# A decoder block on one core: list schedule with other costs, and four of eight groups of the first MLP layer as seven block products

## The chip, the cores and the metric

One core of one Trainium2 chip. The metric is the device time of one execution in microseconds (us), the median of several runs. Everything is float32; there are no collectives.

## The reference, cut to what matters

A decoder block for 512 tokens and 1024 channels, one layer: a conditioning vector gives shifts, scales and gates; a mixer (convolution branch and attention branch, merged by gates) and then an MLP each add to the residual stream.

```python
h = rms_norm(x, g_pre_mix) * (1.0 + scale1) + shift1
y = token_mixer(h, ...)                          # convolution (31 taps), latent attention (8 heads), output projection
x = x + gate1 * rms_norm(y, g_post_mix)
h = rms_norm(x, g_pre_mlp) * (1.0 + scale2) + shift2
y = jnp.square(jax.nn.relu(h @ w_mlp_in)) @ w_mlp_out     # (512 x 1024)(1024 x 4096), then (512 x 4096)(4096 x 1024)
x = x + gate2 * rms_norm(y, g_post_mlp)
```

In the token mixer the latent rows are normed as `rms_norm(q_lat)` (384 wide) and `rms_norm(kv_lat)` (256 wide); that is `lat_norm` in the kernel.

## The kernel before, in words

**Matmuls.** Every large product is made in three passes: both operands are split into a high part in the rounded type float32r (a cast, on ACT) and a low part (value minus high part, a subtraction on DVE); `mm3` (L454) adds high*high, high*low and low*high. Class `W` (L472) splits a loaded weight tile of 1024 words a partition: one cast on ACT, one subtraction on DVE. Split operands live in `r_arena` (28000 words a partition), unsplit data and loaded weights in `f_arena` (22400 words); PSUM has 8 banks.

**Order.** The program is first only recorded: each operation becomes an `Op` with a cost by `Planner.cost` (L217), its regions read and written by `region` (L195), and its dependencies (`record`, L245). `plan` (L306) is a list scheduler: it gives each operation a deadline, counted back from the PE operations that need it, and lets five queues (PE, ACT, DVE, POOL, SP) run in simulated time; PE takes what is ready in program order, the others by deadline (less a bonus `hurry`). DMA is modelled by 475 ns of issue and one channel of 360 bytes per ns. `lives` (L366) gives the times from which to which each buffer was in use; the arenas place buffers by them in the next pass. After at most `PASSES` passes (L47, L1603) the shortest plan is issued, one instruction after another, by `issue` (L385): hence all instructions have line L388. Each engine runs its queue in that order. A pass that finds no room in an arena ends the search.

```python
    for _ in range(PASSES):
        try:
            plan = emit(plan.lives(), {})
        except MemoryError:
            break
        plan.plan()
        if plan.length < best.length:
            best = plan
```

**The MLP.** `h2` (L1406 and after) holds the normed and modulated tokens as 8 split pairs of 128 channels x 512 tokens: 8192 words of `r_arena`. Tokens come in two halves (`tp`), each of 4 x 2 PSUM pieces of 256 columns; a piece is scaled on ACT, cast on ACT and subtracted on DVE. The hidden layer is worked in four chunks of 8 blocks of 128 hidden channels (`for ch`, L1527). In a chunk:
- the first layer takes two groups of four blocks (8 groups in all; chunk 0 takes four blocks at a time, the others two and two). A block is 8 channel tiles x 3 matmuls of 512 token columns; a group is loaded by four DMAs of 512 KB (`hid_weights`, L1369) and split as four `W`. ACT then takes relu out of PSUM and squares. The very first group runs in two steps of 256 columns, since the second half of the tokens is ready later.
- the second layer of the chunk (512 tokens x 1024 hidden x 1024 channels) is made by `strassen` (L1447): both operands in 2 x 2 blocks, seven products of blocks in place of eight, with sums of blocks formed on DVE in `f_arena` and split afterwards. A product is 2 x 4 x 3 = 24 matmuls of 512 columns and has three split pairs of 1024 words as its operands (one of the hidden values, two of the weights), which are given back after it; `banked` adds its result out of PSUM to the output rows, on DVE or, the first time, by a copy on ACT.

**lat_norm** (L867): for each of four token tiles two squares with a sum (ACT), two scalings (ACT), two powers of -1/2 (POOL, one column each), two multiplies (ACT); then transposes on PE.

The functions that the diff touches:

Of the kernel before, what the change touches and what calls it, by code (L numbers as in the profile page):

```python
# [17 lines left out]
P = 128  # L18
# [28 lines left out]
PASSES = 8  # L47
LEAD = 15000.0
ADAS = (1, 1, 0, 4)
# [117 lines left out]
class Planner:  # L167
# [6 lines left out]
    def __init__(self, nc, spaces):  # L174
        self.spaces = spaces
        self.real = dict(pe=nc.tensor, act=nc.scalar, dve=nc.vector, pool=nc.gpsimd, sp=nc.sync)
        self.ops = []
        self.last_w = {}
        self.reads = {}
        self.boost = 0  # L180
        self.hurry = 0.0
        self.after = None

# [11 lines left out]
    def region(ap):  # L195
# [5 lines left out]
        if row == 0 or len(t.shape) < 2 or "dram" in name or "spill" in name:  # L201
            return name, range(0, 1)
# [5 lines left out]
        return name, range(lo // u, hi // u + 1)  # L208

# [7 lines left out]
    def cost(self, eng, fn, outs, ins, k):  # L217

        n = max(self.free_size(o) for o in (ins if fn == "reduce_sum" else outs))
        if fn == "dma_start":  # L220
            return 475.0, 2000.0
        psum = any(r.tensor.name.startswith("psum") for r in ins + outs)
        if eng == "pe":
            if fn == "transpose":
                return 0.85 * n + 1, 190.0
            if ins[0].dtype == F32:
                return max(53.5, n / 2.4 + 2) * 4, 190.0
            return max(64.0, n / 2.4 + 2.5), 190.0
        scalars = sum(isinstance(v, bass.AP) and self.free_size(v) == 1 for v in ins) if n > 1 else 0
        if eng == "act":  # L230
            t = 0.833 * n + (51 if psum else 93) + 93 * scalars
# [13 lines left out]
    def record(self, eng, fn, a, k):  # L245
# [16 lines left out]
        o.cost, o.post = self.cost(eng, fn, outs, ins, k)  # L262
        if fn == "dma_start":
            b = 4
            for _, c in outs[0].ap:
                b *= c
            o.dma = b
# [38 lines left out]
    def plan(self):  # L306
# [8 lines left out]
        for o in reversed(ops):  # L315
            lat = o.post + (o.dma / 180.0 if o.dma else 0.0)
# [5 lines left out]
        dma_free = 0.0  # L322
        future = []
# [10 lines left out]
        while len(order) < len(ops):  # L334
# [3 lines left out]
            for e in self.NAMES:  # L338
                if free[e] <= now and heaps[e]:
# [53 lines left out]
def tile_hybrid_block(  # L393
# [48 lines left out]
    def emit(past, replay):  # L442
# [424 lines left out]
        def lat_norm():  # L867
            for t in range(NT):
                s = stat(4)
                j = ra.alloc(QL)  # L870
                act.activation(ra.v(j), fa.v(latF[t])[:, 0:QL], AF.Square, accum_out=s[:, 0:1])
                act.activation(ra.v(j)[:, 0:KL], fa.v(latF[t])[:, QL:QL + KL], AF.Square, accum_out=s[:, 1:2])
# [3 lines left out]
                act.mul(fa.v(latF[t])[:, 0:QL], fa.v(latF[t])[:, 0:QL], s[:, 2:3])  # L876
                act.mul(fa.v(latF[t])[:, QL:QL + KL], fa.v(latF[t])[:, QL:QL + KL], s[:, 3:4])
# [472 lines left out]
        h2 = []  # L1350
# [23 lines left out]
        for tp in range(2):  # L1374
# [30 lines left out]
            if tp == 0:  # L1405
                h2[:] = [pair(T) for _ in range(KD)]  # L1406
            hsl = slice(tp * 256, (tp + 1) * 256)
            for k2 in range(KD // 2):
# [5 lines left out]
                for q in range(2):  # L1414
                    k = 2 * k2 + q
                    ps, v = pb.v(b)[:, q * 256:(q + 1) * 256], fa.alloc(256)
                    hb, lb = h2[k]
                    if k == 0:
                        act.activation(ra.v(hb)[:, hsl], ps, AF.Identity, scale=mod[:, 3, k:k + 1], bias=mod[:, 2, k:k + 1])
                        dve.tensor_scalar(fa.v(v), ps, mod[:, 3, k:k + 1], mod[:, 2, k:k + 1], ALU.mult, ALU.add)  # L1420
                    else:
                        act.activation(fa.v(v), ps, AF.Identity, scale=mod[:, 3, k:k + 1], bias=mod[:, 2, k:k + 1])
                        act.copy(ra.v(hb)[:, hsl], fa.v(v))
                    dve.tensor_tensor(ra.v(lb)[:, hsl], fa.v(v), rf(hb)[:, hsl], ALU.subtract)
                    fa.free(v)
# [100 lines left out]

        for ch in range(NCH):  # L1527
# [3 lines left out]
            for n0 in range(0, HPC, GRP):  # L1531
                bs = [pb.alloc() for _ in range(GRP)]
# [17 lines left out]
            if ch == NCH - 1:  # L1550
                for p_ in h2:
# [92 lines left out]
```

## Time and profile before

| | |
|---|---|
| runs, us | 822.37, 822.44, 826.56 |
| median, us | 822.44 |
| the profiled execution, us | 821.15 |
| its span (first to last instruction), us | 819.4 |
| busy, us (share of the span) | PE 799.6 (98%), DVE 685.5 (84%), ACT 423.3 (52%), POOL 28.5 (3%) |
| PE instructions | 3934 matmuls seen |
| DMA | 117.28 MB, mean 143 GB/s |
| granted TensorE clock | 0.997 of full speed |

PE is TensorE's matmuls, PEld its weight loads (which overlap them), DVE is VectorE, ACT ScalarE, POOL GpSimd, SP the engine whose queue issues the DMAs. All times below are counted from the first instruction of the span. Matmuls are pipelined: the duration of one in a row is longer than the distance from its start to the next one's. The profiler misses a few matmuls, so counts of them can be a little low.

### The profile page before, as it was taken

Reading aid. Unit: us, or ns where it says so; the run is one execution under the profiler, and the core shown is the slowest. Engines: PE = TensorE matmul, PEld = TensorE weight load, DVE = VectorE, ACT = ScalarE, POOL = GpSimd, SP = SyncE. Lnnn points to the kernel's source line nnn. Section 1 sums busy time; section 2 is a strip of 40 time slices with the busy share of each in tenths; the row PEclk is TensorE's granted clock in tenths of the full one; section 3 lists DMA queues with packets and bytes.
Section 4 is the critical chain, followed back from the end, with each engine's and each line's share of the span. In section 5 each row is a group of like instructions: output and inputs, shape, how many; then the busy total and the mean of one; then the engine's idle time right before and its main releaser. Section 6 shows DMA issues by size and latency. Waiting matters only on the chain.

```text
span 819.4 us, 10628 instructions
## 1 busy us (share of the span) xinstructions
PE 799.6 (98%) x3934; PEld 673.5 (82%) x3934; DVE 685.5 (84%) x1014; ACT 423.3 (52%) x714; POOL 28.5 (3%) x84
## 2 busy tenths in 40 slices
PE   6999999999999999999999989999999999999995
PEld 4778988899988888888888889888888888888884
DVE  4989899999999999989999798397539993975696
ACT  5373554375894255228334496465345434553552
POOL 2001210000000000000000020000000000000001
PEclk9999999999999999999999999999999999999998
DMA  9997324202263151134799660173015831660302
GB/s 305 330 336 256 126 76 122 80 1 77 79 206 103 27 154 52 52 98 154 255 325 385 239 188 26 52 227 108 0 52 165 283 117 52 201 209 1 103 0 104
DMA packets 87111, 117.28 MB, mean 143 GB/s; under 512 B 7345, under 2 KB 61970, under 8 KB 87058
## 3 DMA queue, kind: packets, MB, share of 16 engines
q1 hardware_dynamic: 87058, 116.59, 44.1%
q8 instruction: 31, 0.51, 0.3%
q14 instruction: 22, 0.18, 0.1%
HBM read 108.18 MB, written 8.39 MB: 142 GB/s over the span
## 4 chain that ended last, share of the span: by engine, by line
PE 95%; ACT 2%; DVE 1%; POOL 1%; DMA 0%; issue 0%; DVEq 0%; ACTq 0%
PE psum L388 95%; DVE f_arena L388 1%; ACT f_arena L388 1%; POOL stats L388 1%; ACT r_arena L388 0%; DMA f_arena<-in_x_dram 0%; ACT stats L388 0%; DVEq L1639 0%; DVE mod L388 0%; ACTq L388 0%
## 5 line engine op out<-in xcount | busy, mean ns | idle before, releaser
L388 PE MATMUL psum<-r_arena 128*128 128x512 f32 (+2 forms) x3592 | 761.5, 372 | 3.2 <-ACT r_arena L388 3.1
L388 PEld LDWEIGHTS psum<-r_arena 128*128 128x128 f32 x3592 | 632.5, 188 | 114.8 <-ACT r_arena L388 3.8
L388 DVE TENSOR_TENSOR r_arena<-f_arena,r_arena 128x1024 fp32r<-128x1024 f32 (+4 forms) x234 | 247.7, 1081 | 92.1 <-PE psum L388 57.6
L388 ACT CAST r_arena<-f_arena 128x1024 fp32r<-128x1024 f32 (+4 forms) x224 | 210.2, 959 | 179.4 <-PE psum L388 117.8
L388 DVE SCALAR_TENSOR_TENSOR f_arena<-f_arena,cw 128x512 f32<-128x512 f32 x240 | 164.9, 744 | 0.0
L388 ACT ACTIVATE f_arena<-psum 128x512 f32<-128x512 f32 x64 | 38.1, 597 | 120.0 <-PE psum L388 119.8
L388 DVE TENSOR_TENSOR f_arena<-f_arena 128x1024 f32<-128x1024 f32 (+3 forms) x78 | 77.0, 1003 | 5.8 <-ACT f_arena L388 3.6
L388 ACT ACTIVATE f_arena<-f_arena 128x512 f32<-128x512 f32 (+4 forms) x100 | 58.5, 604 | 18.6 <-DVE f_arena L388 17.4
L388 DVE SCALAR_TENSOR_TENSOR f_arena<-f_arena,cT 128x256 f32<-128x256 f32 (+2 forms) x84 | 55.3, 699 | 0.1
L388 PE MATMUL psum<-ident,f_arena 128*128 128x128 f32 x234 | 34.9, 286 | 7.6 <-DVE f_arena L388 7.6
L388 PEld LDWEIGHTS psum<-ident,f_arena 128*128 128x128 f32 x234 | 28.8, 147 | 13.0 <-DVE f_arena L388 8.4
L388 DVE TENSOR_TENSOR f_arena<-psum,f_arena 128x512 f32<-128x512 f32 x52 | 35.5, 684 | 4.6 <-PE psum L388 4.4
L388 DVE TENSOR_TENSOR r_arena<-psum,r_arena 128x512 fp32r<-128x512 f32 (+2 forms) x57 | 35.7, 656 | 1.7 <-ACT r_arena L388 1.0
L388 POOL TENSOR_TENSOR stats<-stats,nhalf 128x1 f32<-128x1 f32 x24 | 20.1, 842 | 476.2 <-ACT stats L388 476.2
L388 ACT CAST r_arena<-psum 128x512 fp32r<-128x512 f32 (+2 forms) x57 | 30.1, 566 | 11.1 <-PE psum L388 10.7
L388 ACT COPY f_arena<-psum 128x512 f32<-128x512 f32 (+5 forms) x42 | 19.8, 500 | 17.6 <-PE psum L388 17.6
L388 ACT ACTIVATE r_arena<-f_arena 128x512 fp32r<-128x512 f32 (+3 forms) x20 | 13.0, 651 | 18.3 <-DVE f_arena L388 16.0
L388 DVE CUSTOM_DVE_ANT_0 f_arena<-psum,mask 128x128 f32<-128x128 f32 (+3 forms) x32 | 15.2, 485 | 2.7 <-PE psum L388 2.5
L388 ACT ACTIVATE f_arena<-f_arena,lnh 128x512 f32<-128x512 f32 x16 | 12.2, 808 | 6.8 <-DVE f_arena L388 6.7
L388 DVE TENSOR_SCALAR f_arena<-f_arena,stats 128x1024 f32<-128x1024 f32 x8 | 6.0, 751 | 10.5 <-POOL stats L388 10.5
L388 DVE SCALAR_TENSOR_TENSOR f_arena<-f_arena 128x512 f32<-128x512 f32 (+1 forms) x18 | 13.2, 743 | 0.2 <-ACT f_arena L388 0.2
L388 DVE SCALAR_TENSOR_TENSOR f_arena<-f_arena,psum 128x512 f32<-128x512 f32 x16 | 10.7, 679 | 0.0
(94 smaller groups left out, 180.3 us busy)
## 6 DMA issues: line engine op xcount, KB each, us to landing
f_arena<-in_w_ada_dram SPq DMA_DIRECT2D x16, 1024.0 KB, 5.3
f_arena<-in_w_mlp_in_dram SPq DMA_DIRECT2D x32, 512.0 KB, 4.4
f_arena<-in_w_mlp_out_dram SPq DMA_DIRECT2D x32, 512.0 KB, 5.4
f_arena<-in_w_in_dram SPq DMA_DIRECT2D x24, 512.0 KB, 4.1
f_arena<-in_x_dram SPq DMA_DIRECT2D x8, 512.0 KB, 5.4
f_arena<-in_w_ada_dram SPq DMA_DIRECT2D x16, 256.0 KB, 5.6
f_arena<-in_w_ada_dram SPq DMA_DIRECT2D x8, 512.0 KB, 7.1
h_spill<-r_arena SPq DMA_DIRECT2D x16, 256.0 KB, 3.8
```

Source lines behind the costliest of these rows:

```text
L388: getattr(self.real[o.eng], o.fn)(*o.a, **o.k)
```

## The change

First, the scheduler's model:
- a matmul of n columns costs max(109, n/2.4 + 13.3) ns in place of max(64, n/2.4 + 2.5); a float32 one of a single column 213 ns; ACT's sine 900 ns more.
- a DMA takes 375 ns of issue, and time on its channel by the contiguous run of its access pattern (`run`); at most eight are in flight (`DEPTH`): the SP queue is held until the eighth last has landed.
- DRAM tensors and spills are told apart by offset (`region`), so pieces that don't overlap no longer depend on each other in the plan.
- up to 14 passes in place of 8; operations on POOL recorded while `plan.slack` is set count as done 4 us later.

Second, `lat_norm` squares all four tiles first and takes one scaling and one power of eight columns.

Third, in four of the eight groups of the first MLP layer (`SIN`: the second group of chunk 0, both of chunk 1, the second of chunk 2) `strassen_in` makes the group by seven products of 2 x 2 blocks: 256 hidden x 512 channels by 512 channels x 256 tokens. Each takes 2 x 4 x 3 matmuls of 256 columns. To that end the modulated tokens are also kept unsplit (`h2f`, two tiles of 2048 words of `f_arena`) until `h2_sums` has made four sums of token blocks, each split into a pair of 1024 words (`h2s_`), which stay until the last such group. The weight sums are made for each group on DVE, and its results are put together by copies (ACT), adds out of PSUM (DVE) and relu and square (ACT). The loads of a group stay four of 512 KB.

```diff
-PASSES = 8
+SIN = ((0, 4), (1, 0), (1, 4), (2, 4))
+DEPTH = 8
+PASSES = 14
 LEAD = 15000.0
+SLOW = 4000.0
...
-            return name, range(0, 1)
+            return name, range(ap.offset, ap.offset + 1)
...
-            return 475.0, 2000.0
+            return 375.0, 2000.0
...
-                return max(53.5, n / 2.4 + 2) * 4, 190.0
-            return max(64.0, n / 2.4 + 2.5), 190.0
+                return (213.0 if n == 1 else max(53.5, n / 2.4 + 2) * 4), 190.0
+            return max(109.0, n / 2.4 + 13.3), 190.0
...
+        o.post += self.slack if eng == "pool" else 0.0
...
-            o.dma = b
+            n = min(self.run(outs[0]), self.run(ins[0]), 4096)
+            o.dma = b * (13.0 + 0.0385 * n) / (16 * n)
...
-            lat = o.post + (o.dma / 180.0 if o.dma else 0.0)
+            lat = o.post + (2.0 * o.dma if o.dma else 0.0)
...
-                        dma_free = st + o.dma / 360.0
-                        o.t1 = dma_free + 910.0
+                        dma_free = st + o.dma
+                        o.t1 = dma_free + 1100.0
+                        landed.append(o.t1)
+                        free[e] = max(free[e], landed[-DEPTH])
...
         def lat_norm():
+            s = stat(4 * NT)
             for t in range(NT):
-                s = stat(4)
...
-                rstd(s[:, 2:3], s[:, 0:1], 1.0 / QL)
-                rstd(s[:, 3:4], s[:, 1:2], 1.0 / KL)
...
+            plan.slack = SLOW
+            rstd(s[:, 2 * NT:], s[:, :2 * NT], 1.0)
+            plan.slack = 0.0
...
+                h2f[:] = [fa.alloc(4 * T) for _ in range(2)]
...
+        def h2_sums():
+            Y = {(j, i): k4(fa.v(h2f[j]))[:, :, 256 * i:256 * i + 256] for j in range(2) for i in range(2)}
+            for nm, o, a, b in ((3, (0, 1), (1, 1), (0, 1)), (1, (0, 0), None, (0, 0)), (2, (1, 1), (1, 1), (0, 0)),
+                                (4, (1, 0), (1, 0), (1, 1))):
+                if nm == 1:
+                    dve.tensor_tensor(Y[0, 0], Y[1, 1], Y[0, 0], ALU.subtract)
+                    dve.tensor_tensor(Y[0, 0], Y[0, 0], Y[0, 1], ALU.subtract)
+                else:
+                    dve.tensor_tensor(Y[o], Y[a], Y[b], ALU.subtract)
+                hl = pair(1024)
+                act.copy(k4(ra.v(hl[0])), Y[o])
+                dve.tensor_tensor(k4(ra.v(hl[1])), Y[o], k4(rf(hl[0])), ALU.subtract)
+                h2s_[nm] = hl
+            fa.free(*h2f)
...
+        def strassen_in(hv, n0, c0):
...
+            def product(xb, y, b, first):
+                w = W(fa.v(xb, "p (k n) -> p k n", k=4), 4, 256)
...
+                for m in range(2):
+                    for k in range(4):
+                        mm3(pb.v(b)[:, m * 256:(m + 1) * 256], w(k, m * P, P), ys_[k], first and m == 0 and k == 0, k == 3,
+                            skip_group_check=True)
+                w.free()
...
+            def keep(i, n, b):
+                act.copy(o(i, n), ps(b))
+
+            def done(i, n, b):
+                v = o(i, n)
+                dve.tensor_tensor(v, ps(b), v, ALU.add)
+                act.activation(v, v, AF.Relu)
+                act.activation(v, v, AF.Square)
+
+            x11, x12 = x_(0, 0), x_(0, 1)
+            ba, bb, bc_ = (pb.alloc() for _ in range(3))
+            product(x11, (0, 0), ba, True)
+            keep(0, 0, ba)
+            product(x12, (1, 0), bc_, True)
+            done(0, 0, bc_)
+            pb.free(bc_)
+            x21, x22 = x_(1, 0), x_(1, 1)
+            s1, s2 = fa.alloc(1024), fa.alloc(1024)
+            sub(s1, x21, x22, ALU.add)
+            sub(s2, s1, x11)
+            product(s2, 2, ba, False)
+            keep(0, 1, ba)
+            product(s1, 1, bb, True)
+            fa.free(s1)
+            keep(1, 1, bb)
+            sub(x21, x11, x21)
+            fa.free(x11)
+            product(x21, 3, ba, False)
+            fa.free(x21)
+            done(1, 1, ba)
+            sub(x12, x12, s2)
+            fa.free(s2)
+            product(x12, (1, 1), bb, False)
+            fa.free(x12)
+            done(0, 1, bb)
+            pb.free(bb)
+            product(x22, 4, ba, False)
...
             for n0 in range(0, HPC, GRP):
+                if (ch, n0 - n0 % 4) in SIN:
+                    if n0 % 4 == 0:
+                        if not h2s_:
+                            h2_sums()
+                        strassen_in(hv, n0, (ch * HPC + n0) * P)
...
+                    continue
```

## Rows read from the trace of the kernel before

**Rows 1.** The page, busy us (share of the span) and instructions of each engine.

```profile
span 819.4 us, 10628 instructions
...
PE 799.6 (98%) x3934; PEld 673.5 (82%) x3934; DVE 685.5 (84%) x1014; ACT 423.3 (52%) x714; POOL 28.5 (3%) x84
```

**Rows 2.** The chain that ended last, in order: start us, us, what.

```profile
by line: PE psum L388 94.9%; DVE f_arena L388 1.4%; ACT f_arena L388 0.9%; POOL stats L388 0.7%; ACT r_arena L388 0.4%; DMA f_arena<-in_x_dram 0.4%; issue 0.3%; ACT stats L388 0.1%; DVEq L1639 0.1%; DVE mod L388 0.0%; ACTq L388 0.0%
...
7.19 36.36 PE psum L388 x174
...
44.81 197.30 PE psum L388 x1131
...
242.77 190.97 PE psum L388 x866
...
434.91 23.97 PE psum L388 x112
...
481.39 329.38 PE psum L388 x1545
```

**Rows 3.** Windows: stretch, its us, busy us (instructions) by engine, PEclk, DMA share, GB/s.

```profile
280.00:300.00 20.00, 20.00 (x90) 16.57 (x89) 19.66 (x26) 8.52 (x10) 0.00 (x0) 1.00 0.54 160
...
320.00:340.00 20.00, 20.00 (x90) 16.57 (x89) 20.00 (x30) 5.45 (x7) 0.00 (x0) 1.00 0.10 27
...
460.00:480.00 20.00, 18.09 (x88) 14.41 (x87) 14.18 (x18) 11.73 (x28) 4.79 (x7) 1.00 0.43 146
```

**Rows 4.** Timeline of PE, end of the MLP: start us, us, operation, count.

```profile
799.49 11.27 PE L388 MATMUL psum<-r_arena 128*128 128x512 f32 x49
```

**Rows 5.** Timeline of PEld, first group of the MLP (256 columns a matmul).

```profile
481.39 7.50 PEld L388 LDWEIGHTS psum<-r_arena 128*128 128x128 f32 x62 [0.25 <-DVE f_arena L388]
```

**Rows 6.** Groups by form, PEld: count | busy us, mean ns | idle before.

```profile
L388 PEld LDWEIGHTS psum<-r_arena 128*128 128x128 f32 x3592 | 632.5, 188 | 114.8 <-ACT r_arena L388 3.8 <-DVE r_arena L388 0.5 <-issue 0.4
```

**Rows 7.** Timeline of DVE: subtractions of 1024 words, multiplies of 512.

```profile
500.52 4.63 DVE L388 TENSOR_TENSOR f_arena<-f_arena 128x1024 f32<-128x1024 f32 x4
...
563.54 3.72 DVE L388 TENSOR_TENSOR r_arena<-f_arena,r_arena 128x1024 fp32r<-128x1024 f32 x3 [0.99 <-ACT f_arena L388]
...
800.68 1.88 DVE L388 TENSOR_TENSOR f_arena<-f_arena 128x512 f32<-128x512 f32 x3
```

**Rows 8.** Timeline of ACT: a pass out of PSUM, casts.

```profile
510.67 0.60 ACT L388 ACTIVATE f_arena<-psum 128x512 f32<-128x512 f32 x1 [3.06 <-PE psum L388]
...
531.07 2.01 ACT L388 CAST r_arena<-f_arena 128x1024 fp32r<-128x1024 f32 x2
```

**Rows 9.** Windows by stages of the MLP, engines in the order of rows 3.

```profile
core 0: us, PE busy (x) PEld busy (x) DVE busy (x) ACT busy (x) POOL busy (x), PEclk, DMA share, GB/s
489.00:565.80 76.80, 76.80 (x405) 66.33 (x404) 56.45 (x58) 47.52 (x68) 0.00 (x0) 1.00 0.36 112
565.80:647.40 81.60, 81.60 (x362) 67.57 (x361) 54.74 (x55) 38.96 (x46) 0.00 (x0) 1.00 0.31 97
647.40:729.00 81.60, 81.60 (x362) 67.57 (x361) 64.90 (x65) 40.58 (x46) 0.00 (x0) 1.00 0.49 159
609.30:647.40 38.10, 38.10 (x170) 31.55 (x169) 36.49 (x39) 23.15 (x23) 0.00 (x0) 1.00 0.59 187
489.00:527.70 38.70, 38.70 (x237) 34.78 (x236) 22.31 (x26) 20.15 (x37) 0.00 (x0) 1.00 0.09 25
481.40:810.60 329.20, 329.20 (x1545) 276.42 (x1545) 241.67 (x247) 172.16 (x228) 2.67 (x3) 1.00 0.34 109
```

**Rows 10.** Waits, who for whom: us in total, times, longest us.

```profile
DVE r_arena L388 <- PE psum L388: 57.6, 14, 14.1
```

**Rows 11.** The page, DMA issues: count, KB each, median us to landing.

```profile
f_arena<-in_w_mlp_in_dram SPq DMA_DIRECT2D x32, 512.0 KB, 4.4
```

**Rows 12.** Groups of POOL: count | busy us, mean ns | idle before.

```profile
L388 POOL TENSOR_TENSOR stats<-stats,nhalf 128x1 f32<-128x1 f32 x24 | 20.1, 842 | 476.2 <-ACT stats L388 476.2
L388 POOL TENSOR_TENSOR lns<-lns,nhalf 128x4 f32<-128x4 f32 x1 | 1.4, 1407 | 253.9 <-DVE lns L388 253.9
```

More of the change, by code (lines that the diff above doesn't have):

```diff
@@ L182, in __init__ @@
         self.after = None
+        self.slack = 0.0
     class Engine:
@@ L208, in region, with run @@
         return name, range(lo // u, hi // u + 1)
+    @staticmethod
+    def run(ap):
+        dims = [list(d) for d in ap.ap]
+        if ap.tensor.name.split("_bitcast")[0].endswith("arena") or dims[0][0] == 0:
+            dims = dims[1:]
+        n = 1
+        for s, c in reversed(dims):
+            if s != n:
+                break
+            n *= c
+        return 4 * n
     @staticmethod
@@ L322, in plan @@
         dma_free = 0.0
+        landed = [0.0] * DEPTH
         future = []
@@ L1349, in emit, with k4 @@
             xr.append(b)
-        h2 = []
+        h2, h2f, h2s_ = [], [], {}
+        def k4(a):
+            return a.rearrange("p (k t) -> p k t", k=4)
         def yl(t, k):
@@ new lines, in strassen_in, with x_, sub, o @@
+        def strassen_in(hv, n0, c0):
+            def x_(i, j):
+                return load(1024, w_mlp_in[512 * j:512 * j + 512, c0 + 256 * i:c0 + 256 * i + 256]
+                            .rearrange("(k p) n -> p k n", p=P), "p (k n) -> p k n", k=4)
+            def sub(o, a, b, op=ALU.subtract):
+                dve.tensor_tensor(fa.v(o), fa.v(a), fa.v(b), op)
+            def product(xb, y, b, first):
+                w = W(fa.v(xb, "p (k n) -> p k n", k=4), 4, 256)
+                if isinstance(y, tuple):
+                    ys_ = [h2s(4 * y[0] + k, 256 * y[1], 256) for k in range(4)]
+                else:
+                    ys_ = [tuple(k4(ra.v(q))[:, k] for q in h2s_[y]) for k in range(4)]
+                for m in range(2):
[3 more added lines that the diff above has]
+                w.free()
+            def o(i, n):
+                return hv[:, n0 + 2 * i:n0 + 2 * i + 2, 256 * n:256 * n + 256]
+            def ps(b):
+                return pb.v(b, 512, "p (m t) -> p m t", m=2)
+            def keep(i, n, b):
[33 more added lines that the diff above has]
+            product(x22, 4, ba, False)
+            fa.free(x22)
+            v = o(1, 0)
+            act.activation(v, ps(ba), AF.Relu)
+            act.activation(v, v, AF.Square)
+            pb.free(ba)
@@ L1531, in emit @@
             for n0 in range(0, HPC, GRP):
+                if (ch, n0 - n0 % 4) in SIN:
[3 more added lines that the diff above has]
+                        strassen_in(hv, n0, (ch * HPC + n0) * P)
+                        if ch >= NCH - 2:
+                            take(late, 2 * ADAS[1])
+                        if (ch, n0) == SIN[-1]:
+                            for nm in list(h2s_):
+                                ra.free(*h2s_.pop(nm))
+                    continue
                 bs = [pb.alloc() for _ in range(GRP)]
@@ L1550, in emit @@
             if ch == NCH - 1:
-                for p_ in h2:
+                for p_ in h2 + list(h2s_.values()):
                     ra.free(*p_)
```

27 lines of the change are left out of this document (14 added, 13 removed).

## The prediction

> **What bounds the kernel now.** I read the page's busy times first: PE is busy 98% of the span, DVE 84%, ACT 52% [rows 1]. A busy PE need not be at its peak, so the chain that ended last came next. It is PE for 95%, in three long stretches, and the pieces between them are short: 1.26 us up to 44.81 us, 0.66 at 242 us, 1.17 at 434 us, and a change of hands between ACT, POOL and DVE from 458.9 to 481.4 us, in which PE itself stood still for 20.00 - 18.09 = 1.9 us [rows 2, 3]. Then I asked how fast PE goes where it doesn't wait: 49 matmuls of 512 columns in 11.27 us, the last of them 0.39 us long, so (11.27 - 0.39) / 48 = 226.7 ns from start to start [rows 4]; at 256 columns 62 weight loads, one per matmul, in 7.50 us, the last 0.19 us, so 7.31 / 61 = 119.8 ns [rows 5]. From 481.39 us on, 329.38 us of chain are PE without a break [rows 2]: the MLP is bound by the number and width of matmuls, and nothing waits there. The first matmul comes at 7.19 us, the last ends at 810.77 of 819.4.
>
> **1. Seven products in place of eight.** A group of four blocks took 4 x 8 x 3 = 96 matmuls of 512 columns: 96 x 226.7 = 21.76 us. Now it takes 7 products x 2 x 4 x 3 = 168 of 256 columns: 168 x 119.8 = 20.13 us. The work falls by an eighth (2.72 us), but the narrower form gives 1.09 us back. Four groups: -4 x 1.63 = **-6.5 us**, all on the path, since PE sets the end there. The first group of the MLP already runs this form (same operands, 256 columns), so the price is measured, not guessed.
>
> A rule against this edit: what if each weight load stuck out behind a stream that short? One load lasts 188 ns [rows 6], and if each were waited for, a group would take 168 x 188 = 31.6 us. The row shows 119.8 from start to start, shorter than one load, so loads overlap. The Trainium skill, "TensorE: Matmul & The Clock Gate", section "LDWEIGHTS (loading the stationary operand)", gives about one column per 1.2 GHz cycle, and its section on weight-path modes leaves fp32 out of the fast load. By that the load alone is about 107 ns (an estimate from that page), as long as the stream, and uncovered it would turn the gain into a loss; the trace's 119.8 ns says it is covered.
>
> **2. What DVE and ACT get to do.** DVE prices by start to start: a 128x1024 subtraction (4.63 - 1.22) / 3 = 1.14 us, a 512-column one (1.88 - 0.68) / 2 = 0.60 us [rows 7]. Each changed group adds three low halves (7 splits for 4), four block sums and three adds out of PSUM: 7 x 1.14 + 3 x 0.6 = 9.8 us. The token sums, made once in chunk 0, add 5 subtractions and 4 low halves: 9 x 1.14 = 10.3 us. In all 49.5 us. ACT: 16 more casts at 2.01 / 2 = 1.0 us and 12 more passes of 512 columns at 0.6 us, 23.2 us [rows 8]; it is busy 172 us of the last 329 [rows 9], so this hides behind PE; a cast that came late would cost what a late low half costs, below.
>
> Whether DVE hides too is the question of this case. I cut the MLP at its stages (a group 21.8 us, a second layer 38.1 us, counted back from the last matmul) and asked for the busy times of each stretch [rows 9]:
> - Chunk 0, 489.0 to 565.8: DVE 56.45 us of 76.8. After: 56.5 + 20.1 = 76.6 in 75.2. **Over its room by 1.4 us.**
> - Chunk 1: 54.7 of 81.6. After: 74.3 in 78.3, 95%.
> - Chunk 2: 64.9 of 81.6, after 74.7 in 80.0, 93%; 8 of its operations feed the last gate alone and can slip into chunk 3.
> What cover there is: from 320 to 340 us DVE is busy 20.00 of 20 us and PE 20.00 too, so a full DVE alone does not stop PE; from 460 to 480 us DVE is busy only 14.18 [rows 3], 5.8 us into which sums and splits could move; and the last three subtractions of chunk 0, 3.7 us from 563.54 us on [rows 7], split weights for chunk 1 and can slip. Bounds: at the best 0. At the worst DVE gets 97% of the time, as in 280 to 300 us (19.66 of 20) [rows 3], so chunk 0 lacks 76.6 - 0.97 x 75.2 = 3.7 us, and chunk 1, with these 3.7 us put on it, 78.0 - 0.97 x 78.3 = 2.0 us: 5.7 us. I take **+1.5 us**, nearer to the lower end, because in chunk 1 of before the second layer ran DVE at 36.49 of 38.1 with PE dense [rows 9].
>
> **3. Room for operands.** The first layer's weights come by the same four 512 KB loads per group, same 1 KB runs. But the four token sums hold 8 x 1024 words of the 28000 of r_arena from chunk 0 to the last changed group, in chunk 2, beside 8192 for h2: 11 tiles of 1024 stay, where there were 19. A second-layer product takes 6. That leaves five of the next product's six to be written early; DVE already waits on PE for such tiles 14 times, 57.6 us in all, the longest 14.1 us [rows 10]. Taken at 0; with the cover gone it is the third rival. The float copy of h2 holds 4096 of f_arena's 22400 words until the token sums are made; loads that this puts off have room, with the DMA engines at a share of 0.09 there [rows 9]: 0, and if not, a 512 KB load of 4.4 us [rows 11] late once. In the first layer a PSUM bank is written again after one product on another bank: 24 x 119.8 = 2.9 us of cover for one 0.6 us eviction.
>
> **4. The list schedule.** Its costs now say 226.6 ns for a matmul of 512 columns where they said 215.8, its DMA knows run lengths and eight in flight, and DRAM regions no longer chain transfers that don't touch. Deadlines and places change in the whole kernel, queues of SP and POOL included. The trace of before can't price this. Upper bound of the gain: the breaks above, 1.26 + 0.66 + 1.17 + 1.9 = 5.0 us. Bound of the loss: breaks as large as the ones there are, 5.0 us, since the same kind of order made them. I take **-1.0 us**: PE is dense over 197 and 191 us already, so nothing more is to be had there, and the break at 458.9 to 481.4 is a chain of dependent small steps that no order shortens.
>
> **5. lat_norm.** 8 ACT scalings and 8 POOL powers of one column become one each of eight; a one-column power takes 0.84 us, one of four columns 1.41 [rows 12], so eight in one go take about 2.2 us, against 6.7. It lies under the conv stage, where POOL idles and PE has its next tiles. All four tiles now wait for one power, some 2 us longer for the first; the GLU products in PE's queue cover that, and without them it would cost these 2 us once: 0. The 4 us that the plan books on top of that power only move its users back in the order.
>
> **6. The tail**, 8.6 us behind the last matmul [rows 2], keeps its operations; a row multiply of 0.6 us [rows 7] may change places with another, either way: 0.
>
> **Sum.** -6.5 + 1.5 - 1.0 = -6.0. The profiled execution lasted 821.15 us (span 819.4), so 815.15 for it; the median of the runs is 822.44, 1.29 above the profiled one. Against the median: **816.4 us**. Faster or slower by 0.5% is 4.1 us, about what a measurement of this kernel can tell.
>
> **Rivals.**
> - *The schedule takes all breaks too.* -6.5 - 5.0 = -11.5: 811 us. For it: the costs are now those of the trace. Against: the breaks are dependencies. Chance 0.14.
> - *DVE becomes the bound of chunks 0 and 1.* With the full 5.7 us lost and nothing from the schedule: 822.44 - 6.5 + 5.7 = 821.6, no change. For it: 76.6 us of work in 75.2. Against: the idle 5.8 us before. Also here: the search ends at the first pass that finds no room, and keeps an early order. Chance 0.21.
> - *Operands no longer fit (slower).* The sixth tile of a product is freed when the running product has read its first weights for the last time, 6 matmuls or 1.36 us before its end, and is read 7 matmuls or 1.59 us into the next: 2.95 us for one low half of 1.14. Two DVE operations ahead of it in the queue make 3.42, 0.5 late; three make 4.56, 1.6 late. Two and three in turn, over the 14 products of chunks 0 and 1: 14 x 1.05 = 14.7 us, 822.44 - 6.5 + 14.7 = 830.6. It decides from 0.76 us per product (10.6 / 14). For it: DVE would be 95% busy, and its queue is in order. Against: before, with six more tiles in reserve, no PE gap at all. The Trainium skill, "Perfetto Trace Analysis", section "Optimization Strategy", reads one gap that repeats on the busiest engine as a sign that the next tile had no room; no such gap is in this trace. Chance 0.11.
> - *Weight loads uncovered* (above): +39 us. Chance 0.01.
>
> **How the numbers follow.** The forecast (816.4, its own range 814 to 819) has 0.53. Faster by over 0.5% (under 818.3): the first rival's 0.14 and the forecast's without a tenth, 0.48: 0.62. Slower (over 826.6): the third and fourth, 0.12. Same: the second and that tenth, 0.26. The range runs from 810, the first rival's 811 less one multiply in the tail, to 823.5, past the second's 821.6 by the 2 us that chunk 2 could lose in the same way; it leaves out the third, the fourth and some of the edges.
>
> **What would show it.** PE matmuls: 384 of 512 columns fewer, 672 of 256 more, at 120 ns from start to start. The chain from about 480 us on: PE alone; if not, DVE r_arena pieces in it, in chunk 0's second layer for the second rival, and one gap per product in chunks 0 and 1 for the third. DVE busy near 735 us in all. The forecast is wrong if the MLP's PE stretch does not fall by 4 us or more, or if breaks of over 2 us appear ahead of 480 us.

## The result, and the profile after

The changed kernel takes 816.0 us (median of five runs, 814.87 to 817.37) against 822.44 (five as well, 820.79 to 826.56); the ratio over all runs is 0.991, 95% interval 0.9889 to 0.9932. 816.4 was forecast. The number came out right, but three of its terms were off by 1 to 1.6 us and cancelled. The kernel before was timed again beside the later runs, with medians of 824.10, 823.17 and 823.90 us; each ratio below is to the runs beside it, and its profiled execution, at 821.15 us, is one of its faster ones. The profiled execution of the changed kernel took 814.87 us, its span 813.09 against 819.37: 6.28 us less.

The page of the kernel after, beside [rows 1]:

```profile
span 813.1 us, 11298 instructions
...
PE 794.8 (98%) x4222; PEld 680.6 (84%) x4222; DVE 731.6 (90%) x1063; ACT 441.4 (54%) x735; POOL 23.7 (3%) x77
```

DVE rose by 46.1 us; the prediction said "near 735", and it is 731.6. PE's groups by form (count | busy us, mean ns | idle before), of before and after:

```profile
L388 PE MATMUL psum<-r_arena 128*128 128x512 f32 x2866 | 665.9, 391 | 1.5 <-ACT r_arena L388 1.5
L388 PE MATMUL psum<-r_arena 128*128 128x256 f32 x418 | 55.2, 285 | 1.7 <-ACT r_arena L388 1.6
```

```profile
L410 PE MATMUL psum<-r_arena 128*128 128x512 f32 x2482 | 580.3, 392 | 1.2 <-ACT r_arena L410 1.2
L410 PE MATMUL psum<-r_arena 128*128 128x256 f32 x1090 | 136.2, 284 | 0.6 <-ACT r_arena L410 0.4 <-DVE f_arena L410 0.2
```

384 wide ones fewer and 672 narrow ones more, to the matmul. The mean durations (392, 284 ns) are no prices: by them a group of 168 narrow matmuls would cost more than one of 96 wide ones. The price is the distance from start to start, as in [rows 4, 5].

The chain that ended last, of the kernel after, beside [rows 2] (start us, us, what):

```profile
by line: PE psum L410 87.9%; DVE f_arena L410 3.9%; ACT f_arena L410 1.8%; DVE r_arena L410 1.7%; ACT r_arena L410 1.6%; POOL stats L410 0.9%; issue 0.8%; DMA f_arena<-in_x_dram 0.5%; ACT stats L410 0.3%; DVEq L1766 0.1%; DVE mod L410 0.1%;
...
34.10 122.49 PE psum L410 x633
...
196.82 6.28 DVE f_arena L410 x15
...
215.94 27.47 PE psum L410 x173
...
244.07 215.80 PE psum L410 x982
...
496.19 301.28 PE psum L410 x1680
...
797.49 0.70 DVE f_arena L410
```

The break at 434 us is gone, as one would wish; but from 157 to 216 us, where PE ran without a break before, the chain now goes over DVE. In the MLP, PE stands alone from 496.19 to 797.47 us. The last 8 us before its last matmul ends (805.61) the chain goes over the small steps of the output rows on DVE, ACT and POOL, where in before it was PE up to the end of the last matmul at 810.77. The new order does that, not the four groups: the new schedule without them leaves PE 8.1 us before its last matmul ends too, and the four groups under the old schedule don't.

**Where the 6.28 us are.** For this and for all runs below I add up, in PE's timeline, the distance from each matmul's start to the next less the price of its form ([rows 4, 5]; those of other forms likewise): these are the breaks, a slow clock included. The stretch runs from the start of the first split matmul to the end of the last, the head is what lies ahead of it, the tail what lies behind it.

| us | head | stretch | breaks 20 to 460 | 460 to 505 | 505 to the end | tail |
|---|---|---|---|---|---|---|
| before | 21.63 | 789.13 | 4.74 | 3.47 | 0.09 | 8.61 |
| after | 21.92 | 783.69 | 5.45 | 3.34 | 0.48 | 7.48 |
| schedule and lat_norm alone | 23.36 | 793.01 | 9.77 | 2.37 | 0.10 | 7.43 |
| the same, four groups narrow | 23.65 | 797.49 | 9.10 | 2.36 | 0.15 | 7.44 |
| seven products, old schedule | 23.79 | 785.23 | 4.80 | 5.89 | 0.17 | 8.63 |
| after, old lat_norm | 22.62 | 791.70 | 12.51 | 3.45 | 1.21 | 7.50 |
| the same, powers booked later | 23.79 | 787.89 | 9.43 | 3.46 | 0.49 | 7.67 |
| after, old DRAM regions | 23.24 | 784.00 | 5.42 | 3.35 | 0.77 | 8.97 |
| after, 2048 words held | 22.93 | 786.25 | 5.21 | 2.69 | 3.86 | 7.45 |
| after, five groups | 23.40 | 782.86 | 5.27 | 3.36 | 1.35 | 7.48 |
| after, six groups | 22.59 | 783.11 | 6.56 | 3.35 | 1.95 | 12.19 |
| after, seven groups | 24.29 | 782.77 | 5.74 | 3.35 | 4.45 | 13.11 |

Of the 6.28 us, 5.44 are in the stretch and 1.13 in the tail; the head took 0.29. The stretch lost -384 x 226.7 + 672 x 119.8 = 6.5 us by price and gave 0.97 of it back in breaks. The head goes from 21.92 to 24.29 us among kernels that begin with the same order of work, so stretch and tail are what kernels are compared by.

### The profile page after: what moved, and what is told of

Its sections match the earlier page's. It is cut to its first block, busy times and chain, and to the rows that moved or that the text cites. A ratio compares the mean times of both kernels' runs of the same rounds, so it can differ in the third digit from the quotient of the medians.

```text
span 813.1 us, 11298 instructions
## 1 busy us (share of the span) xinstructions
PE 794.8 (98%) x4222; PEld 680.6 (84%) x4222; DVE 731.6 (90%) x1063; ACT 441.4 (54%) x735; POOL 23.7 (3%) x77
## 4 chain that ended last, share of the span: by engine, by line
PE 88%; DVE 6%; ACT 4%; POOL 1%; issue 1%; DMA 0%; DVEq 0%; ACTq 0%
PE psum L410 88%; DVE f_arena L410 4%; ACT f_arena L410 2%; DVE r_arena L410 2%; ACT r_arena L410 2%; POOL stats L410 1%; DMA f_arena<-in_x_dram 0%; ACT stats L410 0%; DVEq L1766 0%; DVE mod L410 0%; DVEq L410 0%; ACTq L410 0%
## 5 line engine op out<-in xcount | busy, mean ns | idle before, releaser
L410 PE MATMUL psum<-r_arena 128*128 128x512 f32 (+3 forms) x3880 | 756.1, 355 | 1.8 <-ACT r_arena L410 1.7
L410 PEld LDWEIGHTS psum<-r_arena 128*128 128x128 f32 x3880 | 640.2, 189 | 100.3 <-ACT r_arena L410 3.4
L410 ACT CAST r_arena<-f_arena 128x1024 fp32r<-128x1024 f32 (+4 forms) x240 | 224.1, 964 | 184.4 <-PE psum L410 133.2
L410 DVE TENSOR_TENSOR r_arena<-f_arena,r_arena 128x1024 fp32r<-128x1024 f32 (+4 forms) x250 | 265.7, 1090 | 38.9 <-PE psum L410 13.4
L410 DVE TENSOR_TENSOR f_arena<-f_arena 128x1024 f32<-128x1024 f32 (+3 forms) x99 | 102.7, 1049 | 2.1 <-ACT r_arena L410 1.0
L410 ACT ACTIVATE f_arena<-f_arena 128x512 f32<-128x512 f32 (+4 forms) x112 | 66.6, 606 | 30.5 <-DVE f_arena L410 29.1
L410 ACT ACTIVATE f_arena<-psum 128x512 f32<-128x512 f32 x52 | 30.9, 593 | 65.8 <-PE psum L410 49.8
L410 DVE TENSOR_TENSOR f_arena<-psum,f_arena 128x512 f32<-128x512 f32 x64 | 43.1, 683 | 3.7 <-DMA f_arena<-in_w_mlp_in_dram 3.5
L410 ACT COPY f_arena<-psum 128x512 f32<-128x512 f32 (+5 forms) x54 | 26.9, 517 | 31.1 <-PE psum L410 30.9
L410 POOL TENSOR_TENSOR stats<-stats,nhalf 128x1 f32<-128x1 f32 (+1 forms) x17 | 14.9, 877 | 475.7 <-ACT stats L410 475.7
L410 DVE SCALAR_TENSOR_TENSOR f_arena<-f_arena 128x512 f32<-128x512 f32 (+1 forms) x18 | 13.3, 745 | 0.2
```

The costliest lines, as they stand in the source:

```text
L410: getattr(self.real[o.eng], o.fn)(*o.a, **o.k)
```

## The experiments

**The schedule alone, and the price of the narrow form.** First, no group by seven products, the tokens' pieces given back at once as before; the cost model and lat_norm are the new ones. Second, the same with four groups in two steps of 256 columns.

```diff
-SIN = ((0, 4), (1, 0), (1, 4), (2, 4))
+SIN = ()
...
-                step = 256 if ch == 0 and n0 == 0 else T
+                step = 256 if (ch == 0 and n0 == 0) or (ch, n0 - n0 % 4) in ((0, 4), (1, 0), (1, 4), (2, 4)) else T
```

> The new list schedule and the new lat_norm alone: all eight groups are made by eight products (SIN is empty), the pieces of h2 are transient as before. Theory 1 (PE is the bound, its matmul count and width set the time, the schedule only trades one short break for another): the sum of PE's breaks stays near the 8 us of before, head and tail within 1 us of before, so the time is that of before within 1.5 us. Theory 2 (the schedule is what made it faster): 3 to 6 us under before.

> As the new schedule alone, but the same four groups run in steps of 256 token columns: twice as many matmuls of half the width, no product saved. Theory 1 (the narrow form costs 119.8 ns where half a wide one is 113.4): 4 x (192 x 119.8 - 96 x 226.7) ns = 5.0 us more than the new schedule alone. Rival (the width costs nothing of its own): the same time as the new schedule alone. Weight loads not covered: 4 x 192 x (188 - 113.4) ns = 57 us more.

Measured: 824.64 us, ratio 1.0006 (0.9988 to 1.0024), no gain at all. The breaks were to stay near 8 us and are 12.2 (the one profile even has stretch and tail 2.7 us above before); and 830.25, ratio 1.0064 (1.0042 to 1.0086). Between the two the stretch grows by 4.48 us while breaks fall by 0.63, so the narrow form costs 5.1 us; four groups at 96 x (2 x 119.8 - 226.7) ns make 5.0. The price holds, and so does the wide one.

The schedule's gain (tail 8.61 to 7.43, breaks at the start of the MLP 3.47 to 2.37) is paid back at one place. Timeline of ACT, DVE, POOL and PE there, with the idle time before each and who ended it:

```profile
358.58 2.07 ACT L410 CAST r_arena<-f_arena 128x1024 fp32r<-128x1024 f32 x2 [4.21 <-DMA f_arena<-in_w_conv_out_dram]
...
359.66 1.23 DVE L410 TENSOR_TENSOR r_arena<-f_arena,r_arena 128x1024 fp32r<-128x1024 f32 x1 [2.30 <-ACT r_arena L410]
360.81 0.15 DVE L410 TENSOR_TENSOR lns<-lns 128x4 f32<-128x4 f32 x1
...
361.04 1.99 POOL L410 TENSOR_TENSOR lns<-lns,nhalf 128x4 f32<-128x4 f32 x1 [251.80 <-DVE lns L410]
...
363.50 3.65 PE L410 MATMUL psum<-f_arena,ones 128*128 128x128 f32 x16 [2.68 <-DVE lns L410]
```

The window behind it (PEclk, the granted clock, is the third figure from the end):

```profile
364.00:368.00 4.00, 4.00 (x21) 3.82 (x20) 2.35 (x5) 1.02 (x4) 0.00 (x0) 0.64 0.00 0
```

Read upwards from PE: it waits for a layer norm's small steps, POOL's power among them; they wait behind a weight's low half on DVE (a queue in order), that for its cast on ACT, and the cast for a weight load that came late. The load itself has nothing to do with the layer norm. Behind the break the 16 matmuls start 213 ns apart, about twice the distance in before, and the granted clock of the window is 0.64. In the kernel after, this break isn't there: the same cost model, with other work in the list, gave another order.

**Seven products under the old schedule.** The cost model, the regions, eight passes and lat_norm are those of before; only the four groups are new.

```diff
-            return max(109.0, n / 2.4 + 13.3), 190.0
+            return max(64.0, n / 2.4 + 2.5), 190.0
...
-            n = min(self.run(outs[0]), self.run(ins[0]), 4096)
-            o.dma = b * (13.0 + 0.0385 * n) / (16 * n)
+            o.dma = b
...
-            return name, range(ap.offset, ap.offset + 1)
+            return name, range(0, 1)
```

> The four groups by seven products under the old cost model, old DRAM regions, 8 passes and the old lat_norm. Theory 1 (PE is the bound and DVE hides): 6.5 us under before, PE without breaks over 0.5 us from the first full group of the MLP to its end. Theory 2 (DVE has no room in chunks 0 and 1, and only the corrected order hides it): breaks of 3 to 6 us in all in the second layers of chunks 0 and 1, so 0 to 3 us under before.

Measured: 818.62 us, ratio 0.9936 (0.9912 to 0.9959), 5.3 us faster; by the profiles the stretch is 3.90 us shorter, 6.5 by price less 2.6 of breaks. From 505 us on there are 0.17 us of breaks, fewer than in the kernel after: the old order hides DVE's added work as well. The theory that the corrected order is what hides it has fallen. What this kernel loses lies just ahead, at the start of the MLP, where the granted clock behind the break is 0.50 as well (484 to 487 us). Why ACT is late there wasn't followed up:

```profile
483.21 0.51 PE L407 MATMUL psum<-r_arena 128*128 128x256 f32 x2 [4.05 <-ACT f_arena L407]
```

**How much DVE can take.** Five, six and seven groups in place of four; only the list changes.

```diff
-SIN = ((0, 4), (1, 0), (1, 4), (2, 4))
+SIN = ((0, 4), (1, 0), (1, 4), (2, 4), (3, 0))
...
+SIN = ((0, 4), (1, 0), (1, 4), (2, 4), (3, 0), (3, 4))
...
+SIN = ((0, 4), (1, 0), (1, 4), (2, 0), (2, 4), (3, 0), (3, 4))
```

> Seven of eight groups by seven products (all but the first, whose weights are split early): three more groups in chunks 2 and 3. Theory 1 with DVE always hidden: 3 x 1.63 = 4.9 us under the changed kernel, 811 us. Theory 2 (DVE's room is the limit): DVE's work from chunk 0 on becomes 241.7 + 10.3 + 7 x 9.8 = 321 us against some 318 us of PE; chunk 3 gets 58.4 + 19.6 + 9.1 = 87 us in 78.3, so PE breaks of 4 to 9 us appear in chunk 3's second layer and the time is 815 to 820 us.

> A fifth group, the first of chunk 3. Theory 1 (DVE's time is the limit, with seven groups it is passed, with five not): DVE has 58.4 + 9.8 = 68 us of 80 in chunk 3, so all of 1.6 us is gained, PE breaks in chunks 2 and 3 stay under 1 us in all, and the tail stays 7.5 us behind the last matmul. Theory 3 (room for operands is the limit; the token sums now stay through chunk 2's second layer): breaks of 2 us or more in chunk 2's second layer.

> The version with a fifth group, now timed. Theory 1 (PE's matmuls set the time, DVE has room for this one): 1.6 us under the changed kernel, ratio to before 0.989. Rival (what the group saves is given back): the same time as the changed kernel.

> Six groups: both of chunk 3 besides the four, chunk 2 as in the changed kernel. Theory 2 (DVE's time is the limit: chunk 3 gets 58.4 + 19.6 us of work in 78.3, and 9.1 more that feeds the last gate): 3.3 us of matmuls saved, but breaks and a longer tail of 3 to 7 us in chunk 3, so 0 to 4 us above the changed kernel. Theory 1 without that limit: 3.3 us under it.

> The changed kernel once more, beside the versions with five and six groups on the same chip. Theory 1: 0.991 of the kernel before, as in the first measurement; PE's breaks between 500 us and the last matmul under 0.6 us in all.

Measured: seven 821.53 us (0.9973, 0.9961 to 0.9985); six 819.68 (0.995, 0.9931 to 0.9969); five 814.59 (one execution), then a median of 815.14 (0.9892, 0.9869 to 0.9915), beside the kernel after at 816.67 (0.9912, 0.989 to 0.9935). Seven is 1.5 us above the upper bound of its second theory. Windows from 500 us to the last matmul (stretch, us, busy us of PE, PEld, DVE, ACT, POOL) for no group, four, five, six and seven; for the last two also chunk 3, and for seven chunk 2:

```profile
500.00:816.40 316.40, 316.28 (x1434) 263.14 (x1433) 230.78 (x231) 160.90 (x207) 1.44 (x2) 1.00 0.32 106
```

```profile
500.00:805.60 305.60, 305.60 (x1687) 266.99 (x1685) 272.00 (x271) 179.51 (x228) 1.44 (x2) 1.00 0.35 111
```

```profile
500.00:806.20 306.20, 306.18 (x1770) 270.26 (x1769) 282.71 (x283) 185.78 (x236) 1.44 (x2) 1.00 0.34 112
```

```profile
500.00:805.70 305.70, 305.12 (x1846) 272.81 (x1844) 288.01 (x287) 190.01 (x242) 0.42 (x1) 1.00 0.34 111
...
725.00:805.70 80.70, 80.70 (x511) 73.24 (x509) 79.72 (x85) 51.87 (x77) 0.42 (x1) 1.00 0.27 92
```

```profile
645.00:725.00 80.00, 78.27 (x502) 70.61 (x501) 79.94 (x80) 46.78 (x56) 0.00 (x0) 1.00 0.48 158
725.00:807.00 82.00, 81.61 (x509) 73.56 (x507) 81.91 (x87) 50.88 (x75) 0.00 (x0) 1.00 0.27 90
500.00:807.00 307.00, 304.85 (x1922) 275.50 (x1920) 296.73 (x297) 193.51 (x247) 0.00 (x0) 1.00 0.34 110
```

DVE's share goes 73, 89, 92, 94, 97%. Up to 92% it is nearly free (breaks 0.10, 0.48, 1.35 us). At 94% what DVE can't do in time doesn't yet show as gaps of PE, which is 80.70 us busy of 80.70 in the last chunk, but behind the last matmul: DVE is late with work that PE doesn't read (adds out of PSUM, row multiplies), and does it at the end. In chunk 3 both groups are changed and DVE is full (79.72 of 80.70 us), while in chunk 2 it has 5.5 us to spare. So it is not the share of the whole MLP alone that decides: behind chunk 3 there is only the tail to slip into. That last step is argued; six groups with fewer in chunk 3 weren't run. Chunk 2, and DVE's last run, in the kernel with six groups:

```profile
647.00:725.00 78.00, 77.98 (x427) 67.66 (x426) 72.49 (x71) 40.72 (x49) 0.00 (x0) 1.00 0.41 135
```

```profile
809.14 5.40 DVE L410 SCALAR_TENSOR_TENSOR f_arena<-f_arena,stats 128x512 f32<-128x512 f32 x8
```

All eight row multiplies stand together behind the MLP, and the tail is 12.19 us in place of 7.48. Seven groups add the gaps, in chunk 2 (78.27 of 80.00), not in chunk 3's second layer. The fifth group saves 0.83 us in the stretch of the profiles, half of its 1.63; the medians differ by 1.5 us with overlapping intervals. It is the fastest version of this study, though its lead on the kernel after is not secure.

**Room in r_arena.** 2048 words are held while the token sums live: 9 tiles of 1024 for products in place of 11.

```diff
+            hold[:] = [ra.alloc(2048)]
             Y = {(j, i): k4(fa.v(h2f[j]))[:, :, 256 * i:256 * i + 256] for j in range(2) for i in range(2)}
...
+                            ra.free(*hold)
                             for nm in list(h2s_):
```

> The changed kernel with 2048 words of r_arena held and never used from the token sums to the last changed group: nine tiles of 1024 stay for operands in place of eleven. Theory 1 (DVE's time is what matters, and the room was more than enough): PE's breaks from 500 us to the end of the MLP stay under 1.5 us in all. Theory 3 (room for operands is the edge): only three of a product's six tiles can be written early, three low halves (3.4 us) then have to be made in about 3 us, so 0.5 to 1.5 us is lost at each of the 14 products of chunks 0 and 1: 7 to 20 us.

Measured: 818.43 us (one execution). Breaks of the MLP 3.86 us for 0.48: neither theory's number. Waits from 505 us to the end of the MLP (us in total, times, longest), in the kernel after and in this one:

```profile
DVE r_arena L410 <- PE psum L410: 10.6, 7, 2.5
...
PEld psum L410 <- DVE r_arena L410: 0.7, 3, 0.3
```

```profile
DVE r_arena L410 <- PE psum L410: 21.4, 11, 6.5
...
PEld psum L410 <- DVE r_arena L410: 4.8, 9, 0.9
```

DVE waits longer until PE has read a tile, and PE waits longer for low halves, as in the third rival, but not product by product. DVE's waits for PE in chunks 0 and 1 lie in the first layers, the last of them before 520.60 and 600.18 us; from there DVE runs without idling, and PE's nine waits come 11.6 to 40.9 us later. Windows of these two stretches:

```profile
520.60:556.70 36.10, 35.70 (x179) 29.61 (x177) 36.10 (x34) 24.99 (x30) 0.00 (x0) 1.00 0.30 92
...
600.20:641.10 40.90, 39.60 (x195) 32.33 (x193) 40.83 (x41) 24.06 (x26) 0.00 (x0) 1.00 0.27 82
```

So what fits is that DVE, held up for want of a tile, loses time that it can't make up in a second layer that fills it. The rival's price was 0.5 or 1.6 us a time; seen are nine waits of 0.9 us at most, 4.8 in all. With 11 tiles there are three, 0.7 us in all. The Trainium skill, "Perfetto Trace Analysis", section "Optimization Strategy", reads the same gap repeated on the engine that should be full as a possible sign of too little room for the next tile. The trace agrees as far as the nine waits came with the loss of room; they are not one gap that repeats at every product.

**lat_norm.** The kernel after with eight powers of one column again; then the same with each of these powers booked 4 us longer in the plan.

```diff
-            s = stat(4 * NT)
             for t in range(NT):
+                s = stat(4)
...
+                plan.slack = SLOW
+                rstd(s[:, 2:3], s[:, 0:1], 1.0 / QL)
+                rstd(s[:, 3:4], s[:, 1:2], 1.0 / KL)
+                plan.slack = 0.0
```

> The changed kernel with the lat_norm of before (eight scalings and eight powers of one column). Theory 1 (it lies under other work): PE's breaks between 150 and 250 us stay as in the changed kernel, some 0.5 us each near 177 and 215 us, and the span moves by under 1 us. Rival (one power for all four tiles makes PE wait there): those two breaks vanish and the span falls by 1 us; the other way, if the batching had helped, it rises by 2 us or more.

> The lat_norm of before under the new schedule, as in the earlier run, but each of its powers is booked 4 us longer on POOL in the plan, as the batched one is in the changed kernel. Theory 4 (the 6 us break near 127 us came of powers that take up to 8.9 us on POOL while DVE runs the convolution, where the plan books 0.6): the break falls under 1.5 us, since work that waits for the powers is ordered later. Rival (eight powers in a row are too slow whatever the order): a break of 4 us or more stays between 110 and 170 us.

Measured, one execution each: 823.59 us, where the kernel before took 823.17 beside it, and 821.12, where it took 823.90. All that the change had gained is gone in the first; the expectation had "2 us or more" as its last case, but no theory for this size. Breaks from 20 to 460 us are 12.51 for 5.45, and with the late booking 9.43. There a break of 3.3 us stays, at 157 us, between what its two theories gave: the place in the order counts, and eight single powers cost even so. Timeline of POOL, ACT and DVE in the first one:

```profile
93.34 9.43 POOL L410 TENSOR_TENSOR stats<-stats,nhalf 128x1 f32<-128x1 f32 x2 [19.26 <-ACT stats L410]
...
102.29 1.03 ACT L410 ACTIVATE f_arena<-f_arena,stats 128x384 f32<-128x384 f32 x2 [8.84 <-POOL stats L410]
...
86.50 15.32 DVE L410 SCALAR_TENSOR_TENSOR f_arena<-f_arena,cw 128x512 f32<-128x512 f32 x23
108.57 1.23 DVE L410 TENSOR_TENSOR r_arena<-f_arena,r_arena 128x1024 fp32r<-128x1024 f32 x1 [6.75 <-ACT r_arena L410]
```

Two powers of one column last 9.43 us, where one by itself takes 0.55 (row in the last section). They end at 102.8, one microsecond behind the end of DVE's 23 operations in a row (86.50 + 15.32 = 101.82). ACT's multiply stands 8.84 us behind them, ACT's queue behind it, and DVE then idles 6.75 us waiting for a cast. The chain that ended last leads from there, over ACT, DVE and a load of `w_uq`, to PE some 25 us later: 3.25 us of break at 127 us, then 13 matmuls at half the clock. In before DVE's run is of 16 operations and ends at 99.85 us. Two powers that began in the middle of it took 1.56 us, and the next two, near its end, 4.19:

```profile
89.17 10.68 DVE L388 SCALAR_TENSOR_TENSOR f_arena<-f_arena,cw 128x512 f32<-128x512 f32 x16
...
92.74 1.56 POOL L388 TENSOR_TENSOR stats<-stats,nhalf 128x1 f32<-128x1 f32 x2 [23.68 <-ACT stats L388]
96.59 4.19 POOL L388 TENSOR_TENSOR stats<-stats,nhalf 128x1 f32<-128x1 f32 x2 [2.29 <-ACT stats L388]
...
103.22 1.23 DVE L388 TENSOR_TENSOR r_arena<-f_arena,r_arena 128x1024 fp32r<-128x1024 f32 x1 [3.37 <-ACT r_arena L388]
```

And after, one power of eight columns, booked late, which nobody stands behind:

```profile
104.59 3.21 POOL L410 TENSOR_TENSOR stats<-stats,nhalf 128x8 f32<-128x8 f32 x1 [31.22 <-ACT stats L410]
```

**DRAM regions.** The kernel after, with all pieces of a DRAM tensor as one region again.

```diff
-            return name, range(ap.offset, ap.offset + 1)
+            return name, range(0, 1)
```

> The changed kernel with the old DRAM regions in the plan (each tensor one unit, so its eight output transfers are chained there). Theory 1 (the tail's 1.0 us between 4.03 us and 3.04 us from the last DVE result to the end is the order of the SP queue, which this sets): the end comes 4.0 us after the last DVE result again, the last two output transfers are issued within 0.4 us of each other. Rival (that 1 us is another of the new costs, or chance): it stays 3.0 us.

Measured: 817.98 us (one execution). The stretch is the same to 0.3 us, the tail 8.97 for 7.48. End of DVE's timeline, after and then here; the last matmul ended at 805.61 and 807.24:

```profile
806.12 0.68 DVE L410 TENSOR_TENSOR f_arena<-psum,f_arena 128x512 f32<-128x512 f32 x1
806.72 1.40 DVE L410 SCALAR_TENSOR_TENSOR f_arena<-f_arena,stats 128x512 f32<-128x512 f32 x2
...
808.65 1.41 DVE L410 SCALAR_TENSOR_TENSOR f_arena<-f_arena,stats 128x512 f32<-128x512 f32 x2
```

```profile
807.66 1.41 DVE L410 SCALAR_TENSOR_TENSOR f_arena<-f_arena,stats 128x512 f32<-128x512 f32 x2
808.99 0.69 DVE L410 TENSOR_TENSOR f_arena<-psum,f_arena 128x512 f32<-128x512 f32 x1
...
811.59 1.41 DVE L410 SCALAR_TENSOR_TENSOR f_arena<-f_arena,stats 128x512 f32<-128x512 f32 x2 [0.43 <-POOL stats L410]
```

The last add out of PSUM starts 0.51 us behind the last matmul in the one, and 1.75 in the other, where two row multiplies of another tile stand ahead of it. So the regions do set the tail here, by DVE's order. But the theory that the run was made for has fallen: from DVE's last result to the end it is 3.21 us, near the 3.03 of after, and not 4.0 again. In before DVE finished 4.58 us behind the last matmul, about as after (4.45), and 4.03 us passed from there to the end (4.05 in the kernel with seven products under the old schedule). That last microsecond goes with the old costs, not with the regions; which of the costs gives it wasn't tried alone.

## Why the prediction was right, and where it was not

- **Step 1, -6.5 us: right.** Counts to the matmul, price to 0.15 us in the narrow kernel and in the result, no weight load uncovered: the fourth rival is out.
- **Step 2, +1.5 us: too much.** Breaks from 505 us on rose by 0.4. The amount of DVE work was right (+46.1 for +49.5); what failed is the step "over its room by 1.4 us", that a chunk must hold its own DVE work. The step also read a row wrongly: 19.66 of 20 us is 98.3%, not 97%. By that its worst case is 76.6 - 0.983 x 75.2 = 2.7 us, all in chunk 0, in place of 5.7, and the second rival's time 818.6 in place of 821.6. Windows of chunks 0 and 1, of chunk 1's second layer, and of chunk 2, beside [rows 9]:

```profile
489.90:564.70 74.80, 74.38 (x466) 67.18 (x467) 72.33 (x73) 53.99 (x75) 0.00 (x0) 1.00 0.31 95
564.70:643.10 78.40, 78.40 (x504) 71.54 (x503) 70.67 (x71) 48.87 (x59) 0.00 (x0) 1.00 0.37 119
643.10:723.10 80.00, 80.00 (x433) 69.70 (x432) 75.35 (x75) 47.54 (x56) 0.00 (x0) 1.00 0.53 169
...
605.00:643.10 38.10, 38.10 (x169) 31.28 (x168) 38.10 (x39) 22.62 (x24) 0.00 (x0) 1.00 0.43 135
```

  Chunk 0 did 72.33 us where 76.6 were put down for it: the rest lay elsewhere. In chunk 1's second layer DVE is busy 38.10 us of 38.10, and PE 38.10 as well. The prediction had the row for it (320 to 340 us in [rows 3]) and still charged 1.5. Work can slip into the next stage while that has room. The last chunk has only the tail behind it, and with six groups the excess is paid there. The second rival is out at four groups; at seven PE does stand still, 1.7 us in chunk 2, with DVE busy 79.94 of 80.00 us.
- **Step 3, 0: right, with little to spare.** Two tiles fewer bring 3.86 us of breaks for 0.48, in nine waits, not in the one gap per product that the third rival had.
- **Step 4, -1.0 us: the sum is nearly right (0.58 - 1.13 = -0.55), its place isn't.** It was to come from breaks ahead of the MLP. These grew by 0.58 us net (0.71 less 0.13); the gain, 1.13, is in the tail. And alone the schedule gives nothing (ratio 1.0006), since a new break of 2.7 us and the slow clock behind it eat the rest. The step "a chain of dependent small steps that no order shortens" failed both ways: the breaks there, from 460 to 505 us, are 3.47 us in before, 2.37 with the schedule alone and 5.89 with seven products under the old one. The first rival, all breaks gone, is out.
- **Step 5, 0: wrong as to what the edit is worth.** It was costed against the old order, with POOL idle and 0.84 us a power [rows 12]. That mean hid the 4.19 us for two. In the new order the old lat_norm costs 8.0 us of stretch (791.70 - 783.69), of it 2.6 by the slow clock; with its powers booked later it costs 4.2 (787.89 - 783.69). What the edit is worth under the old order was not run; without it, batching and booking together, the change would have gained nothing at all.
- **Step 6, 0: wrong by 1.13 us.** Its bound, "a row multiply may change places", looked at DVE's order, which gave 0.13; 1.0 us lies behind DVE's last operation, where the step named nothing.

Chances: the forecast's case held, 816.4 for 816.0. Its signs held as well: the counts, the price, a stretch shorter by 5.44 us, no break over 0.9 us between 20 and 480 us. Only the chain is not PE alone up to the last matmul. But the terms behind step 1 were +1.5 and -1.0 where the stretch gave +1.0, the tail -1.1 and the head +0.3; the agreement to half a microsecond is luck, that to two is not.

## What to carry to other kernels

When a change gives work to an engine beside the bound one, compare the engine's load with the whole stretch in which the work may slip, not with each stage, and remember that the last stage has nothing behind it but the tail; look for the excess behind the last matmul as well as in gaps. A list scheduler's new order must be costed by its worst single place, a small operation behind a large one that waits for a load; and an edit that looks free on the old order may be what the new one stands on. Prices of small operations on POOL are read one by one, beside what DVE does in the same microseconds, not as a mean.

## What was not expected of the hardware

**POOL can stand still beside DVE.** One power of one column is 0.55 us alone:

```profile
5.79 0.55 POOL L388 TENSOR_TENSOR stats<-stats,nhalf 128x1 f32<-128x1 f32 x1 [2.31 <-ACT stats L388]
```

Beside DVE's 23 operations in a row one lasted 8.92 us in the chain that ended last (93.34 to 102.26), until that run was over. The Trainium skill, "SBUF — State Buffer", section "Who interferes with whom", says that a DVE instruction with two inputs in SBUF and a GpSimd instruction that reads SBUF lock each other out for a whole instruction. The trace agrees that POOL loses time, but not on how much: here not one DVE operation of 0.7 us was waited for, but the rest of the run (8.91 us once more with the powers booked later), while in before two powers in the middle of such a run took 1.56 us together. What decides between the two isn't shown, and that it is the lock was not shown by itself.

**A break can cost more than its length, and two alike needn't cost alike.** Windows around the break at 127 us with the old lat_norm, and around the one at 157 us with the powers booked later (PEclk, the granted clock, is the third figure from the end):

```profile
127.00:130.00 3.00, 0.30 (x3) 0.06 (x1) 3.00 (x6) 2.14 (x4) 0.00 (x0) 0.90 0.68 220
130.00:136.00 6.00, 5.61 (x13) 4.45 (x14) 6.00 (x10) 0.00 (x0) 0.00 (x0) 0.50 0.39 91
```

```profile
157.00:161.00 4.00, 0.73 (x7) 0.48 (x5) 4.00 (x9) 0.19 (x1) 0.00 (x0) 1.00 0.18 62
161.00:165.00 4.00, 4.00 (x33) 3.73 (x32) 3.94 (x7) 3.02 (x6) 0.00 (x0) 1.00 0.01 2
```

After 3.1 us without work the granted clock was 0.50 (1.2 of 2.4 GHz) for 13 matmuls, 427 ns each in place of 226.7, which is 13 x 0.2 = 2.6 us more; after 3.3 us without work it stayed at 1.00. Ahead of the first break PE had run 24 transposes of 128 columns, ahead of the second 71 split matmuls without a gap. That alone doesn't decide it: the break with the schedule alone, 2.7 us, came behind split matmuls too, and the clock fell (0.64 in the window shown there). What decides isn't shown.
